# Cross entropy with label smoothing: load buffers moved to multiples of 256 bytes, the first row in three tiles instead of four, the second row loaded into the first row's buffers, the first row's finish moved

One core of one Trainium2 chip. The metric is the device time in microseconds of one execution (the median of several), compared with the kernel before on the same chip.

## The reference, cut to what matters

```python
batch, num_classes = 256, 32000
log_probs = logits - max(logits, row);  log_probs -= log(sum(exp(log_probs), row))
smooth_targets = smoothing / num_classes everywhere, plus 1 - smoothing at the label
loss = -sum(smooth_targets * log_probs, row)          # 256 float32
```

So each row needs the sum of its logits, the sum of their exps, and the logit at its label. The 32.77 MB of logits are read once. Each of the 128 partitions holds two batch rows of 32,000 columns, which the kernel works through one after the other ("first row", "second row").

## The kernel before

A tile of columns of all partitions is loaded; VectorE sums it (as two halves added with an accumulator), ScalarE takes exp with an accumulator. Both write a scratch result that nobody reads.

```python
WIDTHS = (
    (8000, 8000, 8000, 8000),
    (8000, 6272, 4736, 3648, 2688, 2048, 1536, 1216, 1024, 832),
)
RING_MIN = 4736
TURN_MAX = 3648
...
ring = ctx.enter_context(tc.tile_pool(name="ring", bufs=3))   # first pool: starts at byte 16,512
...
def load(w: int, col: int, name: str):
    if w >= RING_MIN:
        xt = ring.tile([P, max(WIDTHS[0])], FP32, name="xt", tag="xt")
    else:
        xt = tail.tile([P, w], FP32, name=name, tag=name)
    if col == 0:
        h = w // 2
        nc.sync.dma_start(out=xt[:, :h], in_=x[:, :h])
        nc.scalar.dma_start(out=xt[:, h:w], in_=x[:, h:w])
    else:
        nc.sync.dma_start(out=xt[:, :w], in_=x[:, col : col + w])
    return xt
...
# after the first row, before the second row's first tile:
#   GpSimd adds the four partial sums (half), ScalarE takes Ln (lse),
#   GpSimd finishes (lin, scaled, loss), TensorE turns the column, VectorE copies it
```

At the end of the second row a last Ln, two transposes on TensorE, two small VectorE operations and the store follow. Ten throw-away matrix products before that (20 matmul instructions in the trace) are meant to keep those transposes short: they take 0.27 us each here, where the first row's transpose, with no such products before it, took 0.37.

The softmax here doesn't subtract the row's maximum and nothing guards it: scores larger than these inputs give would overflow.

## Time and profile before

| | before |
|---|---|
| median of 6 runs | 84.78 us (84.75 to 84.93) |
| span of the profiled execution | 83.2 us |
| busy: DMA queues (sum of the three) / ScalarE / VectorE | 93.3% / 71% / 45% |
| last landing of a load / start of the final Ln | 79.11 us / 80.20 us |

The profiled execution itself took 84.96 us, 0.2 over the median. A "landing" is the last of the sixteen semaphore increments of a transfer, one from each DMA engine. A load runs on all sixteen engines; each engine moves eight partition rows of it, and each row is one packet. The lines that the argument rests on stand in the prediction.

### The profile page before, as it was taken

The page shows a single profiled execution, that of the slowest core. Times are in us where ns is not written, and L with a number is a line of the kernel's source. Part 1 is how long each engine was busy: PE and PEld are TensorE (multiplying, and loading weights), DVE is VectorE, ACT ScalarE, POOL GpSimd, SP SyncE. Part 2 cuts the span into 40 slices and gives each one's busy share as a digit, 9 for nine tenths or more (in the row PEclk, how much of TensorE's full clock was granted, in tenths as well). Part 3 has the DMA queues.
Part 4 walks back from the last instruction along what each step waited for, and adds up shares of the span by engine and source line. Part 5 has one row for each costly group of instructions (what it writes and reads, how often), then busy time and mean ns, then how long its engine had stood idle before and what let it go on. Part 6 is the DMA issues. An engine that isn't in the chain of part 4 may idle for free.

```text
span 83.2 us, 230 instructions
## 1 busy us (share of the span) xinstructions
PE 7.0 (8%) x23; PEld 5.0 (6%) x23; DVE 37.1 (45%) x35; ACT 58.8 (71%) x31; POOL 5.7 (7%) x19
## 2 busy tenths in 40 slices
PE   0000000000000000000000010000000000899020
PEld 0000000000000000000000000000000000787000
DVE  0000005950495009910397017922944736754860
ACT  5000005997499809994399908997999999999960
POOL 3201640031000000000000040000000000000000
PEclk9999999999999999999999999999999999999995
DMA  5999999997999899989998998998999999999600
GB/s 131 416 416 408 454 423 462 477 447 323 477 493 431 369 431 493 446 369 416 493 462 354 416 439 386 495 447 370 428 420 414 442 407 415 412 414 412 256 0 0
DMA packets 2258, 32.77 MB, mean 394 GB/s; under 512 B 337, under 2 KB 338, under 8 KB 850
## 3 DMA queue, kind: packets, MB, share of 16 engines
q1 hardware_dynamic: 2018, 30.72, 87.4%
q10 hardware_dynamic: 144, 2.05, 5.8%
q0 software_dynamic: 96, 0.00, 0.1%
HBM read 32.77 MB, written 0.00 MB: 394 GB/s over the span
## 4 chain that ended last, share of the span: by engine, by line
DMA 64%; ACT 32%; issue 1%; SPq 0%; PE 0%; DVE 0%; ACTq 0%
DMA xt<-in_logits_dram 40%; DMA xl<-in_logits_dram 23%; ACT ja L188 17%; ACT jt L188 15%; SPq L167 0%; PE lse_t L193 0%; DVE res L284 0%; ACT lse L279 0%; ACTq L188 0%
## 5 line engine op out<-in xcount | busy, mean ns | idle before, releaser
L188 ACT ACTIVATE ja<-xt 128x8000 bf16<-128x8000 f32 (+2 forms) x7 | 43.9, 6276 | 20.1 <-DMA xt<-in_logits_dram 20.0
L173 DVE SCALAR_TENSOR_TENSOR jd<-xt 128x4000 f32<-128x4000 f32 (+2 forms) x7 | 27.7, 3954 | 33.6 <-DMA xt<-in_logits_dram 33.6
L188 ACT ACTIVATE jt<-xl 128x3648 bf16<-128x3648 f32 (+6 forms) x7 | 12.2, 1748 | 0.1
L173 DVE SCALAR_TENSOR_TENSOR jd<-xl 128x1824 f32<-128x1824 f32 (+6 forms) x7 | 7.9, 1125 | 5.2 <-DMA xl<-in_logits_dram 5.0
L270 PE MATMUL warm<-xl,ident 128*128 128x256 f32 x20 | 6.1, 471 | 21.4 <-DMA xl<-in_logits_dram 21.4
L270 PEld LDWEIGHTS warm<-xl,ident 128*128 128x128 f32 x20 | 4.8, 246 | 22.5 <-DMA xl<-in_logits_dram 21.7
L193 PE MATMUL loss_t<-ident,loss 128*1 128x128 f32 x1 | 0.4, 372 | 49.2 <-POOL loss L224 49.2
L193 PEld LDWEIGHTS loss_t<-ident,loss 128*1 128x1 f32 x1 | 0.1, 79 | 49.2 <-POOL loss L224 49.2
L226 DVE COPY res<-loss_t 1x128 f32<-1x128 f32 x1 | 0.3, 278 | 4.5 <-PE loss_t L193 4.5
L211 POOL TENSOR_TENSOR half<-sums 128x4 f32<-128x4 f32 x1 | 0.2, 198 | 28.2 <-ACT ja L188 28.2
L125 POOL DMA_INDIRECT gat<-in_logits_dram,flat_idx x2 | 2.0, 1004 | 0.7 <-POOL ident masks.py:199 0.4
L92 ACT ACT_TABLE_LOAD x1 | 1.3, 1283 | 0.9 <-PEq L311 0.9
L188 ACT ACTIVATION_READ_ACCUMULATOR ja<-xt 128x1 f32 x7 | 1.3, 186 | 0.0
L188 ACT ACTIVATION_READ_ACCUMULATOR jt<-xl 128x1 f32 x7 | 1.3, 181 | 0.0
L146 POOL TENSOR_SCALAR weighted<-gat 128x1 f32<-128x1 f32 x1 | 0.8, 763 | 5.8 <-DMA gat<-in_logits_dram,flat_idx 5.8
L105 POOL DMA_DIRECT2D lab<-in_labels_dram x1 | 0.8, 766 | 1.0 <-POOLq L311 1.0
L216 ACT ACTIVATE lse<-half 128x1 f32<-128x1 f32 x1 | 0.2, 203 | 0.6 <-POOL half L211 0.6
L173 DVE DVE_READ_ACCUMULATOR jd<-xt 128x1 f32 x7 | 0.6, 82 | 0.0
L173 DVE DVE_READ_ACCUMULATOR jd<-xl 128x1 f32 x7 | 0.6, 82 | 0.0
L117 POOL TENSOR_TENSOR flat_idx<-rowoff,lab 128x2 int32<-128x2 int32 x1 | 0.2, 197 | 5.4 <-DMA lab<-in_labels_dram 5.4
L193 PE MATMUL lin_t<-ident,done 128*1 128x128 f32 x1 | 0.3, 270 | 3.0 <-DVE done L263 3.0
L282 DVE COPY lin_row<-lin_t 1x128 f32<-1x128 f32 x1 | 0.3, 278 | 0.4 <-PE lin_t L193 0.4
(20 smaller groups left out, 3.8 us busy)
## 6 DMA issues: line engine op xcount, KB each, us to landing
xt<-in_logits_dram SPq DMA_DIRECT2D x4, 4000.0 KB, 21.1
xt<-in_logits_dram SPq DMA_DIRECT2D x1, 3136.0 KB, 19.4
xt<-in_logits_dram SPq DMA_DIRECT2D x1, 2368.0 KB
xt<-in_logits_dram SPq DMA_DIRECT2D x1, 2000.0 KB, 11.5
xt<-in_logits_dram ACTq DMA_DIRECT2D x1, 2000.0 KB, 13.2
xl<-in_logits_dram SPq DMA_DIRECT2D x1, 1824.0 KB, 19.5
xl<-in_logits_dram SPq DMA_DIRECT2D x1, 1344.0 KB, 22.3
xl<-in_logits_dram SPq DMA_DIRECT2D x1, 1024.0 KB, 24.3
```

Of the source, the lines that this page charges most:

```text
L92: nc.scalar.add_instruction(mybir.InstLoadActFuncSet(name=nc.get_next_instruction_name(), act_func_set_id=tbl, ins=[], outs=[],))
L105: nc.gpsimd.dma_start(out=lab[:], in_=labels.bitcast(I32).rearrange("(p f) -> p f", p=P))
L117: nc.gpsimd.tensor_tensor(out=flat_idx[:], in0=rowoff[:], in1=lab[:].rearrange("p (r two) -> p r two", two=2)[:, :, 0:1], op=ALU.add,)
L125: nc.gpsimd.indirect_dma_start(out=gat[:, r : r + 1], out_offset=None, in_=logits[:], in_offset=bass.IndirectOffsetOnAxis(ap=flat_idx[:, r ...
L146: nc.gpsimd.tensor_scalar(out=weighted[r], in0=gat[:, r : r + 1], scalar1=label_weight, scalar2=None, op0=ALU.mult,)
L173: return nc.vector.scalar_tensor_tensor(out=jd[:, :h], in0=xt[:, :h], scalar=1.0, in1=xt[:, h:w], op0=ALU.mult, op1=ALU.add, accum_out=out,)
L188: nc.scalar.activation(out=ja[:, :w], in_=xt[:, :w], func=AF.Exp, accum_out=out)
L193: nc.tensor.transpose(out=row[:], in_=column, identity=ident[:])
L211: nc.gpsimd.tensor_tensor(out=half[:], in0=sums[:, :, :n], in1=sums[:, :, n:], op=ALU.add)
L226: nc.vector.tensor_copy(out=res[:, :, r : r + 1], in_=loss_t[:])
L270: nc.tensor.matmul(warm[:], lhsT=ident[:], rhs=xt[:, i * WARM_COLS : (i + 1) * WARM_COLS], start=True, stop=True,)
L282: nc.vector.tensor_copy(out=lin_row[:], in_=lin_t[:])
```

## The change

Four things at once. The load buffers are moved so that each starts on a multiple of 256 bytes (an unused pad of 384 bytes ahead of them; the first tile's split becomes a multiple of 64 columns). The first row comes in three tiles instead of four, the last of them large (the first tile is still loaded as two halves). The second row comes in eleven; nine of them are loaded into the first row's three buffers, several tiles to a buffer, and the last two have buffers of their own. And the finish of the first row moves behind the second row's first tile, with two scratch places instead of three. A beat is what a DMA engine moves in one cycle of its clock, 32 bytes. The intent: no lost beats in the transfers, and exp and loads in step to the end.

```diff
 WIDTHS = (
-    (8000, 8000, 8000, 8000),
-    (8000, 6272, 4736, 3648, 2688, 2048, 1536, 1216, 1024, 832),
+    (8000, 12480, 11520),
+    (8192, 6336, 4608, 3392, 2496, 1920, 1472, 1152, 960, 768, 704),
 )
-RING_MIN = 4736
-TURN_MAX = 3648
-WARM_LEFT, WARM_COLS = 5, 256
+FOLLOW = (1, 2, 6)
+TURN_MAX = 4608
+PAD = 384
+WARM_LEFT, WARM_COLS = 6, 256
...
-    ring = ctx.enter_context(tc.tile_pool(name="ring", bufs=3))
+    pad = ctx.enter_context(tc.tile_pool(name="pad", bufs=1))
+    pad.tile([nc.NUM_PARTITIONS, PAD // 4], FP32, name="pad", tag="pad")
+    wide = ctx.enter_context(tc.tile_pool(name="wide", bufs=1))
...
-    turn = ctx.enter_context(tc.tile_pool(name="turn", bufs=3))
+    turn = ctx.enter_context(tc.tile_pool(name="turn", bufs=2))
...
+    for r in range(R):                       # FOLLOW: how many second-row tiles share a buffer
+        for b in range(len(FOLLOW)):
+            ...
+            buf = wide.tile([P, w], FP32, name=f"wide{b}_{r}", tag=f"wide{b}")
+            ...buffers.append(buf[:, at : at + v])
...
-            h = w // 2
+            h = w // 128 * 64
...
+        if t == 0:                           # second row, after its first tile's exp
+            finish_first_row(part, exps)
```

## The prediction

> **What bounds the kernel now.** I read the page's 40 slices first, then the chain of work that ended last, then the tail of ScalarE's and VectorE's timeline, then the DMA records. The slices say which resource is never idle. The "DMA" row is the busy share of the 16 DMA engines in tenths:
>
> ```profile
> ACT  5000005997499809994399908997999999999960
> DMA  5999999997999899989998998998999999999600
> ```
>
> and the chain, as shares of the span by engine, is
>
> ```profile
> DMA 64%; ACT 32%; issue 1%; SPq 0%; PE 0%; DVE 0%; ACTq 0%
> ```
>
> The DMA engines are at 7 to 9 tenths from the second slice to the 37th (2.08 us each). ScalarE (exp) has holes through the first row and is full only in the last 13 slices. In the chain, 64% of the span is a transfer, 32% exp. The loads bound the kernel, and exp follows them closely at the end. How closely is in the timeline (start, duration, engine, line):
>
> ```profile
> 40.80 6.87 ACT L188 ACTIVATE ja<-xt 128x8000 bf16<-128x8000 f32 x1 [2.51 <-DMA xt<-in_logits_dram]
> 50.31 6.87 ACT L188 ACTIVATE ja<-xt 128x8000 bf16<-128x8000 f32 x1 [1.75 <-DMA xt<-in_logits_dram]
> 57.77 5.43 ACT L188 ACTIVATE ja<-xt 128x6272 bf16<-128x6272 f32 x1 [0.50 <-DMA xt<-in_logits_dram]
> ...
> 67.72 3.24 ACT L188 ACTIVATE jt<-xl 128x3648 bf16<-128x3648 f32 x1
> ...
> 70.96 2.44 ACT L188 ACTIVATE jt<-xl 128x2688 bf16<-128x2688 f32 x1
> ...
> 78.18 1.06 ACT L188 ACTIVATE jt<-xl 128x1024 bf16<-128x1024 f32 x1
> ...
> 79.24 0.88 ACT L188 ACTIVATE jt<-xl 128x832 bf16<-128x832 f32 x1
> ...
> 80.20 0.26 ACT L279 ACTIVATE lse<-elast,done 128x1 f32<-128x1 f32 x1
> ```
>
> The waits shrink from 2.51 to 0.50 us and then vanish, so the tile widths were already chosen so that each exp ends when the next tile lands. The trace's landing times (the last of a transfer's sixteen semaphore increments) show that the tail is still the loads': landings at 67.69, 70.94, 73.42, 75.31, 76.82, 78.10 and 79.11 us, exp starts 0.02 to 0.13 us after each. The final Ln starts at 80.20, and the rest (two transposes, one VectorE operation, the store) is not touched.
>
> Are transfers ever held up for a free buffer? No: the loads are issued at 20.35, 28.83, 38.32 and 47.79 us, each while one transfer is under way and at least one more is queued behind it; the DMA row never empties. The rate over two of the large transfers, the last column of the windows view, is
>
> ```profile
> 22.00:31.30 9.30, 0.00 (x0) 0.00 (x0) 4.19 (x2) 6.81 (x2) 0.00 (x0) 1.00 1.00 430
> 31.30:40.80 9.50, 0.00 (x0) 0.00 (x0) 4.33 (x2) 6.96 (x2) 0.00 (x0) 1.00 1.00 431
> ```
>
> **What the Trainium skill says.** (1) "DMA: Bandwidth & Descriptors", section "Where 436 GB/s comes from": 16 ports of 32 B at 850 MHz, 435 GB/s. The trace agrees: 430 to 431 above, so about 1% is left here. (2) Same page, "How a descriptor splits into AXI transactions": pieces of 256 B, each starting at a multiple of 256; a descriptor that starts off such a multiple begins at the boundary below and pays beats for bytes it does not use. (3) Same page, "Why small descriptors are slow": about 3 cycles fixed per packet. I tabulated the trace's DMA packets (one per partition row) by size. The shortest durations are 131 ns for 3,328 B, 404 for 10,752 B, 931 for 25,088 B, 1,185 for 32,000 B. The formula (bytes/32 + 3 + 4)/0.85 ns gives 130.6, 403.5, 930.6, 1184.7. The 4 is what a start 128 bytes past a boundary should cost (128/32 beats), and the kernel before does have all load buffers there: its first buffer is placed at byte 16,512 of a partition, 64.5 x 256, and the others follow in multiples of 256. The fit is within 1 ns on four sizes, but it cannot split 7 cycles into 3 and 4; that split is the page's. (4) "ScalarE: Activation LUTs", "What ACT_TABLE_LOAD costs": 186 ns + 0.833 ns per element. The rows by form give 6870 ns for 8000 columns (formula 6850) and 880 for 832 (879).
>
> **The change part by part.**
> *Alignment.* The pad of 384 bytes moves the first load buffer to 16,896 = 66 x 256; all widths are multiples of 64 columns, so all buffers are aligned, and the first split (3968 + 4032 columns instead of 4000 + 4000) aligns the second half at its source too. By point 2 each packet loses 4 cycles, 4.7 ns. There are 15 load transfers (the first is two halves), 8 packets on each engine per transfer, before and after alike: 120 x 4.7 ns = 0.56 us. The last landing goes from 79.11 to about 78.55.
> *Three transfers in the first row instead of four.* One transfer less before the row's end, one more after it; in the total nothing, at the row's end 8 packets of 7 cycles. The first row ends after 32 packets of 3 extra cycles instead of 40 of 7, plus one completion descriptor (about 15 ns) less: (280 - 96)/0.85 + 15 = 0.23 us earlier, so at 40.72 - 0.23 = 40.49 us.
> *Larger tiles in the first row.* The slack moves. The last first-row tile is 11,520 columns rather than 8000, so exp is now behind from 40.5 us on instead of from about 67. Exp steps: 0.833 ns per column, plus the overhead from one start to the next. The 1024-column step before took 79.24 - 78.18 = 1.06 us, of which 0.85 is columns, so 0.21; the mean of the last seven is 0.24, but those waited for landings. I take 0.20 to 0.24. The first step (same scratch written twice running, so it waits for the accumulator read) I put at 0.37, the last at 0.27 (832: 0.96 - 0.69). From 40.49 + 0.08: 43,520 columns x 0.8333 = 36.27; 0.37 + 10 x 0.20 + 0.27 = 2.64; the first row's Ln, now between the second row's first two tiles, 0.20 (its row: 203 ns). Sum: 79.68 us for the final Ln; with 0.24 per step 80.08.
> *Last tile 704 instead of 832 columns.* If the loads end it: 78.55 + 0.08 + 0.59 + 0.27 = 79.49.
> *Buffers that follow.* The second row's tiles go into the first row's three buffers. The 8192 can be issued at about 20.4, 6336 and 4608 when the exp of 12,480 is done (about 37.7), six more at about 50.5; the queue ahead lasts until 40.5, 50.2 and 63.1. No bubble.
> *Scratch 3 to 2, first row's finish moved.* Scratch at a distance of two is long free. The finish leaves the waiting point of 0.58 us (for GpSimd) out of ScalarE's queue, which was hidden before (1.75 us of waiting followed) and would not be now.
> *Sum.* The later of 79.49 (loads) and 79.68 to 80.08 (exp), against 80.20: 0.12 to 0.52 us saved. I choose the middle of the better half, 0.4, so 84.77 - 0.4 = 84.4.
>
> **The rivals.**
> A. *Alignment gives nothing*: the 7 cycles are fixed per packet. For it: the split is not seen in the trace, since every buffer was off by the same 128 bytes. Against: the page's rule fits without a free parameter. Then the row ends at 40.72 - 0.08 = 40.64, exp ends at 79.8 to 80.2, the loads at 79.11 + 0.94 = 80.05: 84.6 to 84.8.
> B. *Exp becomes the bound and eats the gain*: two tiles more in the unbroken chain. For it: my own sum has exp 0.2 to 0.6 us behind the loads. Against: the widths look tuned to keep step. Upper end 84.8.
> C. *False waits between slices of one buffer* (4608 waiting for the exp of 6336): that would stop prefetching and cost several us. Against: slices of one small tile are already written by several engines before, with no such wait in the list of waits. Would give 87 to 95; I give it 2%.
> D. *TensorE cools*: the warming products are 9 x 256 columns instead of 10 x 256 and end at about 75.6 instead of 77.0, with the last transposes near 80. The cold transpose takes longer:
>
> ```profile
> 49.21 0.37 PE L193 MATMUL loss_t<-ident,loss 128*1 128x128 f32 x1 [49.21 <-POOL loss L224]
> ...
> 80.52 0.27 PE L193 MATMUL lse_t<-ident,lse 128*1 128x128 f32 x1 [0.20 <-ACT lse L279]
> ```
>
> So at worst 0.1 us back; included as 0.03.
> E. *More than expected*: misaligned packets may also cause the slower ones (median 935 ns at 25,088 B where the shortest is 931). Removing those too gives up to 0.4 us more of loading, of which exp lets through only what comes before 40 us: 84.0.
>
> **Range and chances.** The centre is 84.4. B and A set the upper end near 84.8; E the lower near 84.0. A gain over 2% needs 83.07, that is 1.7 us; all DMA time above 435 GB/s is (busy 77.35 us, my sum of packet times over 16 engines, against 32.77 MB / 435 GB/s = 75.3) 2.0 us, and exp would have to give way too: 3%. A loss over 2% needs C: 2%.
>
> **What would show it right or wrong.** Right: the shortest packets at (bytes/32 + 3)/0.85, e.g. 935 ns for 25,344 B and 1,839 for 49,920; the first row's exp of 11,520 starting near 40.6; from there ScalarE without waits on a DMA above 0.1 us; the last landing near 78.6 and the final Ln near 79.7. Packets at 7 cycles mean rival A. Exp starts that trail their landings by more than 0.5 us mean B. Loads issued after the exp of a slice-mate mean C. A last transpose of 0.37 us means D. The prediction is wrong outright if the DMA row shows an empty slice before 78 us, or if the span moves more than 1 us either way.

## The result, and the profile after

| | before | after |
|---|---|---|
| median | 84.78 us | 84.30 us (84.21 to 84.64, 6 runs) |
| ratio of fast runs | 1 | 0.9945, 95% interval 0.9926 to 0.9963 |
| span of the profiled execution | 83.2 us | 82.4 us |
| last landing | 79.11 us | 78.53 us |
| start of the final Ln | 80.20 us | 79.50 us |

A ratio here is the mean time of one kernel's fast runs over that of the other's fast runs of the same rounds, so it is not quite the ratio of the medians. The change saves 0.5 us, 0.55%: within 2%, as forecast (84.4, range 84.0 to 84.8). The two profiled spans differ by more (0.8 us) because the profiled execution of before was 0.2 us over its median (84.96 us), that of after 0.1 under (84.22).

The same two rows of the slices and the chain, of the kernel after:

```profile
ACT  5000002999100999992399999999999999999960
DMA  6999999999998889988969969998999999999800
```

```profile
DMA 48%; ACT 47%; issue 1%; SPq 0%; PE 0%; DVE 0%; ACTq 0%
```

The DMA row still has no empty slice until the end. ScalarE's row is solid from the 21st slice rather than from the 29th, and the chain now splits evenly between loads and exp: from the first row's last tile on, it runs through exp. The timeline of ScalarE:

```profile
40.54 9.80 ACT L209 ACTIVATE ja<-wide 128x11520 bf16<-128x11520 f32 x1 [2.88 <-DMA wide<-in_logits_dram]
...
50.47 7.03 ACT L209 ACTIVATE ja<-wide 128x8192 bf16<-128x8192 f32 x1
...
57.50 0.19 ACT L250 ACTIVATE lse<-acc 128x1 f32<-128x1 f32 x1
57.69 5.48 ACT L209 ACTIVATE ja<-wide 128x6336 bf16<-128x6336 f32 x1
...
77.81 0.83 ACT L209 ACTIVATE jt<-tail 128x768 bf16<-128x768 f32 x1
...
78.64 0.77 ACT L209 ACTIVATE jt<-tail 128x704 bf16<-128x704 f32 x1
...
79.50 0.26 ACT L310 ACTIVATE lse<-elast,done 128x1 f32<-128x1 f32 x1
```

After the 2.88 us in front of the 11,520 there is no bracket, so no wait that the profile sees. Yet exp is hardly behind the loads: the trace's landings of the last five tiles (1472, 1152, 960, 768 and 704 columns) are at 74.14, 75.51, 76.69, 77.67 and 78.53 us, and their exps start 0.11 to 0.17 us later. Both keep step to the end.

**The packets.** I tabulated the trace's DMA packets and landings as for the prediction; the profile's printed views do not show them. A row of 25,344 bytes took 940 ns in 110 of its 128 packets, and up to 960 in the rest. Before, 25,088 bytes took 931 at the least, 935 in the median and up to 940. So the *shortest* packet is as far above its beats as before, 7 cycles, where I had said 3; what shrank is how many packets are longer than the shortest. By the test I had set myself this looks like rival A.

But the shortest duration is not the pace. The pace is in the landings: take the mean of the sixteen increments of a transfer, from the end of the first row to the last load. After: 78.38 - 40.28 = 38.10 us, that is 32,381 cycles at 850 MHz (38.095 us before rounding), where 32,000 columns are 32,000 beats for each engine (eight rows of 4 bytes a column, 32 bytes a beat). The trace itself gives that clock: from 2,816 to 49,920 bytes the shortest packets grow from 112 to 1,844 ns, 1.177 ns for 32 bytes. The 381 cycles over are shared by 11 transfers of 8 packets: 4.3 per packet. Before: 78.79 - 40.40 = 38.39 us, 629 cycles over, 80 packets: 7.9. So each packet did become about 3.5 cycles cheaper (7.86 - 4.33).

The mean of the recorded durations shows nearly the same: over the second row's tiles after its first, 10.2 cycles above the beats before, 7.2 after. In both kernels that is 2 to 3 cycles more than the pace, so by these records a packet starts before the one ahead of it is recorded as ended, whether aligned or not.

### The profile page after: what moved, and what is told of

Read it like the earlier page. It is cut to its first block, busy times and chain, and to the rows that moved or that the text cites. A ratio compares the mean times of both kernels' runs of the same rounds, so it can differ in the third digit from the quotient of the medians.

```text
span 82.4 us, 227 instructions
## 1 busy us (share of the span) xinstructions
PE 6.9 (8%) x21; PEld 4.9 (6%) x21; DVE 36.9 (45%) x35; ACT 58.1 (70%) x31; POOL 9.7 (12%) x19
## 4 chain that ended last, share of the span: by engine, by line
DMA 48%; ACT 47%; issue 1%; SPq 0%; PE 0%; DVE 0%; ACTq 0%
DMA wide<-in_logits_dram 48%; ACT ja L209 27%; ACT jt L209 19%; SPq L188 0%; PE lse_t L216 0%; DVE res L315 0%; ACT lse L310 0%; ACT lse L250 0%; ACTq L209 0%
## 5 line engine op out<-in xcount | busy, mean ns | idle before, releaser
L209 ACT ACTIVATE ja<-wide 128x8000 bf16<-128x8000 f32 (+4 forms) x5 | 39.8, 7958 | 20.7 <-DMA wide<-in_logits_dram 20.7
L194 DVE SCALAR_TENSOR_TENSOR jd<-wide 128x4000 f32<-128x4000 f32 (+11 forms) x12 | 34.4, 2870 | 38.9 <-DMA wide<-in_logits_dram 38.9
L209 ACT ACTIVATE jt<-wide 128x4608 bf16<-128x4608 f32 (+6 forms) x7 | 14.6, 2093 | 0.0
L301 PE MATMUL warm<-wide,ident 128*128 128x256 f32 x18 | 6.0, 508 | 11.6 <-DMA wide<-in_logits_dram 11.6
L236 POOL TENSOR_TENSOR acc<-acc,sums 128x2 f32<-128x2 f32 x1 | 4.1, 4127 | 12.6 <-ACT ja L209 12.6
L301 PEld LDWEIGHTS warm<-wide,ident 128*128 128x128 f32 x18 | 4.7, 267 | 12.8 <-DMA wide<-in_logits_dram 11.9
L209 ACT ACTIVATE jt<-tail 128x768 bf16<-128x768 f32 (+1 forms) x2 | 1.6, 800 | 0.0
L209 ACT ACTIVATION_READ_ACCUMULATOR jt<-wide 128x1 f32 x7 | 1.3, 187 | 0.0
L194 DVE SCALAR_TENSOR_TENSOR jd<-tail 128x384 f32<-128x384 f32 (+1 forms) x2 | 1.1, 542 | 0.0
L194 DVE DVE_READ_ACCUMULATOR jd<-wide 128x1 f32 x12 | 1.0, 81 | 0.0
```

The lines of the kernel that those rows point to most:

```text
L194: return nc.vector.scalar_tensor_tensor(out=jd[:, :h], in0=xt[:, :h], scalar=1.0, in1=xt[:, h:w], op0=ALU.mult, op1=ALU.add, accum_out=out,)
L209: return nc.scalar.activation(out=ja[:, :w], in_=xt[:, :w], func=AF.Exp, accum_out=out)
L236: nc.gpsimd.tensor_tensor(out=acc[:], in0=total, in1=sums[:, :, t : t + 1], op=ALU.add)
L301: nc.tensor.matmul(warm[:], lhsT=ident[:], rhs=xt[:, i * WARM_COLS : (i + 1) * WARM_COLS], start=True, stop=True,)
```

## The experiments

Twelve kernels ran, in three groups on three chips; each group shares the runs of the kernel before (medians 84.90, 84.84 and 84.89 us). "Over" is the pace just described: cycles per packet over the beats, second row. "Start" is where the load buffers start, in bytes past a multiple of 256.

| run | start | median us | ratio to before, 95% | last landing us | over |
|---|---|---|---|---|---|
| before | 128 | 84.78 | 1 | 79.11 | 7.9 |
| after | 0 | 84.30 | 0.9945 (0.9926 to 0.9963) | 78.53 | 4.3 |
| a1_before_aligned | 0 | 84.29 | 0.9929 (0.9909 to 0.9950) | 78.59 | 4.3 |
| a2_after_off128 | 128 | 84.76 | 0.9987 (0.9968 to 1.0006) | 79.03 | 7.9 |
| a3_after_off64 | 64 | 84.78 | 0.9993 (0.9969 to 1.0017) | 79.15 | 7.8 |
| a4_after_off192 | 192 | 84.65 | 0.9981 (0.9959 to 1.0002) | 78.88 | 7.9 |
| b1_src_off128 | 0, source at 128 | 84.34 | 0.9935 (0.9921 to 0.9949) | 78.54 | 3.7 |
| b2_src_dst_off128 | 128, source at 128 | 84.69 | 0.9982 (0.9969 to 0.9996) | 78.99 | 7.4 |
| c1_finish_early | 0 | 84.57 | 0.9969 (0.9953 to 0.9984) | 78.55 | 4.8 |
| c2_ln_first | 0 | 88.56 | 1.0441 (1.0425 to 1.0457) | 78.50 | 3.9 |
| d1_half_pieces | 128, one end on a multiple | 84.53 | 0.9953 (0.9938 to 0.9968) | 78.81 | 5.6 |
| d2_exp_half | 0 | 84.30 | 0.9925 (0.9907 to 0.9943) | 78.60 | 4.2 |
| d3_turn3 | 0 | 84.32 | 0.9932 (0.9915 to 0.9948) | 78.49 | 3.9 |
| d4_split_4000 | 0 | 84.23 | 0.9919 (0.9902 to 0.9937) | 78.53 | 4.0 |

(The last landing also depends on how far apart the sixteen engines finish, 0.27 us in a4 and 0.43 to 0.56 in a1 to a3; the pace does not.)

### Which part of the change is it?

**a1**: the kernel before with the alignment alone.

```diff
+    pad = ctx.enter_context(tc.tile_pool(name="pad", bufs=1))
+    pad.tile([nc.NUM_PARTITIONS, 384 // 4], FP32, name="pad", tag="pad")
     ring = ...
-            h = w // 2
+            h = w // 128 * 64
```

> The kernel before with only the 384-byte pad and the aligned first split. Alignment theory (each load packet costs 4 cycles of 0.85 GHz less, 120 packets on each DMA engine, so 0.56 us): last load lands at about 78.55 us instead of 79.11, exp keeps up (its back-to-back overhead is 0.19 us per tile), final Ln near 79.5, time 84.3, 0.5 us under the kernel before. Rival (the gain comes from the widths, the fewer early transfers and the smaller last tile): landings as before, 84.8.

Measured: 84.29 us, and 4.3 cycles over per packet. The whole gain is there without any of the new widths, shared buffers or moved finish. (The final Ln of its profile, of an execution of 84.42 us, is at 79.69 rather than the 79.5 expected.)

**a2**: the changed kernel with the alignment alone taken away.

```diff
-PAD = 384
+PAD = 256
```

> The changed kernel with a pad of 256 bytes, which puts every load buffer 128 bytes past a multiple of 256 again, all else as changed. Alignment theory: last landing near 79.1, time 84.7 to 84.9, the gain is gone; packets spread over several ns again. Rival (widths): 84.3, as the changed kernel.

Measured: 84.76 us; its ratio to before has 1 inside the interval. ScalarE, VectorE and all widths are the same as after; only the start of the buffers differs. The pace is back at 7.9 and the spread too (25,344 bytes: 940 at the least, 945 in the median, 948 at most). a1 and a2 together settle it: alignment gives all of the gain that can be measured, the rest together nothing that the runs can tell from zero. Something small is not excluded: a2's interval leaves room for 0.27 us, and the smaller last tile does bring the final Ln nearer to the last landing (0.97 us after it in a2, 1.09 before).

### What is it about the alignment?

My reason was that a packet pays beats for the bytes below its start. Then the distance must count.

**a3** and **a4**: `PAD = 192` and `PAD = 320`, all else as changed.

> The changed kernel with all load buffers 64 bytes past a multiple of 256. Rule of wasted beats (a packet pays for the bytes below its start): 64/32 = 2 cycles per packet, 120 packets, 0.28 us: last landing 78.8, time 84.55. Rival (any start off the multiple costs the same, one more piece): last landing 79.1, time 84.8.

> The changed kernel with all load buffers 192 bytes past a multiple of 256. Rule of wasted beats: 192/32 = 6 cycles per packet, 0.85 us over the changed kernel: last landing 79.4, time 85.1. Rival (any start off the multiple costs the same): last landing 79.1, time 84.8.

Measured: 7.8 and 7.9 over, like 128 bytes, and 84.78 and 84.65 us. The rule of wasted beats wanted 2 and 6 more cycles than aligned; it falls. Any of the three starts costs the same, 3.5 cycles per packet. (In all three kernels the ends of the rows are off by as much as the starts.)

**b1** and **b2**: move the source instead (b1), or both (b2).

```diff
-    (8000, 12480, 11520),
-    (8192, 6336, ..., 768, 704),
+    (8032, 12480, 11488),
+    (8224, 6336, ..., 768, 672),
     # buffers still rounded up to a multiple of 256 bytes; b2 has PAD = 256 as well
```

> The changed kernel with the first tile of each row 32 columns wider and the last 32 narrower, load buffers still at multiples of 256 bytes: the source in memory of 12 of the 14 later transfers (96 of 120 packets on each engine) now starts 128 bytes past such a multiple, the destination does not. If only the destination counts: 84.3, last landing 78.5, all packets of a size equal. If source and destination count alike: about 4 cycles on 96 packets, 0.45 us: 84.7, last landing 79.0.

> The same columns with the pad of 256 bytes: source and destination both 128 bytes past a multiple of 256. If only the destination counts: 84.75, as with the destination alone. If what counts is that the two are shifted against each other: 84.3. If both count and add: 85.2.

Measured: b1 is as fast as the changed kernel (84.34 us, 3.7 over, all packets of a size equal), b2 is as slow as with the destination alone (84.69, 7.4). Where the row starts in memory, counted from the start of the logits (their own address is in no trace), does not matter here; where it lies in the partition does. Nor does it help that both are shifted alike. (In b2 a packet of 32,896 or 2,688 bytes, which starts 128 past a multiple and *ends* on one, has the same median as in b1. That led to d1.)

**d1**: buffers off by 128 bytes, but tile widths such that one end of nearly every row lies on a multiple, so that no row is cut into more pieces of 256 bytes than its length needs.

```diff
-    (8000, 12480, 11520),
-    (8192, 6336, 4608, 3392, 2496, 1920, 1472, 1152, 960, 768, 704),
-TURN_MAX = 4608
-PAD = 384
+    (8032, 12480, 11488),
+    (8224, 6304, 4640, 3360, 2528, 1888, 1504, 1120, 992, 768, 672),
+TURN_MAX = 4640
+PAD = 256
-            h = w // 128 * 64
+            h = w // 128 * 64 + 32
```

> All load buffers 128 bytes past a multiple of 256 (pad of 256 bytes), but nearly all tiles an odd number of 32 columns wide, so that a row that starts 128 past a multiple ends on one, and the next slice starts on one: off the boundary, yet never cut into more pieces of 256 bytes than its length needs (104 of 120 packets on each engine; 12,480 and 768 columns stay as they were). Theory (the cost is that of one more piece): last landing 78.6, 84.3 to 84.4. Rival (a start off the boundary costs by itself): some 64 of 120 packets start off it, last landing 78.8 to 78.9, 84.6; if an end off it costs as well, 84.8.

Measured: 84.53 us, halfway, and 5.6 over. My theory of the extra piece wanted 84.3 and about 4.3, and falls. The last of the forecasts (start and end each cost) said 84.8, too much. The first rival, that a start off a multiple costs by itself, has the time (84.6) and the landing right, but not tile by tile. Single tiles scatter (in the aligned kernels from about 2 to 7 over, by the place of the transfer in the order), so I compare means, at the same places:

| cycles over per packet | d1 | aligned kernels | a2 to a4 |
|---|---|---|---|
| start off, end on a multiple (8224, 6304, 3360, 1888, 1120) | 5.6 | 3.6 | 8.1 |
| start on, end off (4640, 2528, 1504, 992) | 6.1 | 4.1 | 8.3 |

(The aligned kernels here are after, c2, d2, d3 and d4.) An end off a multiple costs what a start does. What fits all the runs is a price per end of a row that is off a multiple of 256 bytes in the partition, some 2 cycles each. This rule was made after d1, and no run was made to test it; but earlier runs hold tiles with one end off whose pace it was not made from. In b1 the tiles of 8224 and 11,488 columns start on a multiple and end off one (5.9 and 6.1 over); in b2 they start off and end on (6.0 and 5.4). In the aligned kernels these places have 2.8 and 2.5, in a2 to a4 8.0 and 8.5. What the engine does at such an end, no run here shows.

**d4**: the first tile split 4000 + 4000 again, in the aligned kernel.

> The changed kernel with its first tile split 4000 + 4000 again instead of 3968 + 4032. One piece more on 8 of 120 packets at most, 0.04 us: not to be told from 84.3.

Measured: 84.23 us. As expected, not to be told apart; that line of the diff is worth nothing measurable.

### What do the other parts do?

**c1**: the finish of the first row put back before the second row's first tile on all engines (`finish_first_row` called ahead of the loop, without the two orderings).

> The changed kernel with the whole finish of the first row put back before the second row's first tile, on all engines. Theory (exp has no slack after the first row, so GpSimd's sum and the Ln stand in its way): the exp of 8192 starts near 51.05 us instead of 50.47, final Ln 0.4 us later, 84.7. Rival (the loads bind in the end and hide it): 84.3. Here VectorE waits too, so GpSimd's sum should take about 0.2 us.

Measured: 84.57 us against 84.34 for b1, an aligned kernel of the same group, and 84.30 for the changed kernel: the order matters, by 0.2 to 0.3 us rather than 0.4. The timeline:

```profile
50.20 0.19 ACT L209 ACTIVATION_READ_ACCUMULATOR ja<-wide 128x1 f32 x1
...
50.52 0.20 POOL L236 TENSOR_TENSOR acc<-acc,sums 128x2 f32<-128x2 f32 x1 [12.62 <-ACT ja L209]
50.74 0.20 ACT L249 ACTIVATE lse<-acc 128x1 f32<-128x1 f32 x1 [0.36 <-POOL acc L236]
50.79 0.19 POOL L241 TENSOR_TENSOR lin<-acc,weighted 128x1 f32<-128x1 f32 x1
50.85 7.01 ACT L209 ACTIVATE ja<-wide 128x8192 bf16<-128x8192 f32 x1
...
79.80 0.26 ACT L308 ACTIVATE lse<-elast,done 128x1 f32<-128x1 f32 x1
```

ScalarE waits 0.36 us for GpSimd, and the exp of 8192 starts at 50.85 instead of 50.47. Nothing after it makes that up: the final Ln starts at 79.80 instead of 79.50. In the kernel before, the same order cost nothing, since 1.75 us of waiting for a load followed (a1 has it too, and is as fast as after). The new widths create this cost and the moved finish removes it.

**c2**: only the Ln put ahead of that exp; VectorE still sums the 8192 columns first.

```diff
+        if t == 0:
+            finish_first_row(part)        # between sum_logits and sum_exps; the Ln without its ordering
```

> The changed kernel with only the first row's Ln put ahead of the exp of 8192 in ScalarE's queue; VectorE still sums the 8192 columns before its copy. Theory (GpSimd's addition really is held up for 4.1 us while VectorE's sum of two operands runs, as the trace of the changed kernel shows it): Ln at about 54.8, exp of 8192 from 55.0, final Ln 4.3 us later, time 88.5. Rival (the 4.1 us is a wrong record, GpSimd's spans being rough): like the early finish, 84.7.

Measured: 88.56 us, the only run far from the rest. In the trace of the changed kernel one addition on GpSimd of 128 x 2 elements, elsewhere 0.19 us, is shown as 4.13 us long:

```profile
37.74 0.19 POOL L236 TENSOR_TENSOR acc<-sums 128x2 f32<-128x2 f32 x1 [16.21 <-ACT ja L209]
50.57 4.13 POOL L236 TENSOR_TENSOR acc<-acc,sums 128x2 f32<-128x2 f32 x1 [12.63 <-ACT ja L209]
```

It ends with VectorE's sum of 8192 columns (50.22 to 54.65 there). The same in c2, where ScalarE now stands behind it:

```profile
50.17 4.42 DVE L194 SCALAR_TENSOR_TENSOR jd<-wide 128x4096 f32<-128x4096 f32 x1 [3.49 <-DMA wide<-in_logits_dram]
...
50.53 4.12 POOL L236 TENSOR_TENSOR acc<-acc,sums 128x2 f32<-128x2 f32 x1 [12.63 <-ACT ja L209]
...
54.68 0.20 ACT L249 ACTIVATE lse<-acc 128x1 f32<-128x1 f32 x1 [4.28 <-POOL acc L236]
...
54.79 7.01 ACT L209 ACTIVATE ja<-wide 128x8192 bf16<-128x8192 f32 x1
```

ScalarE waited 4.28 us, so the long record is real. This is what the Trainium skill, "SBUF — State Buffer", section "Who interferes with whom", says: a VectorE instruction with two inputs from that memory contends with a GpSimd instruction that reads it, as the second input comes through a shared interface. Here it held GpSimd up for 4.1 us. In c1 VectorE stands behind the copy at that moment, and the same addition takes 0.20 us. So the order of the changed kernel hides a 4 us block: the Ln comes at 57.50 us, when the sum has been ready since 54.70.

**d2**: exp over half the columns of every tile but the last (a wrong result, relative error 0.06).

```diff
+        k = w if w == WIDTHS[1][-1] else w // 2
-        ... out=ja[:, :w], in_=xt[:, :w] ...
+        ... out=ja[:, :k], in_=xt[:, :k] ...
```

> The changed kernel with exp over only half the columns of every tile but the last (wrong result on purpose, same transfers): takes ScalarE off the path until the last tile. Both bind in the changed kernel (exp starts trail their landings by 0.1 us in the tail): final Ln at 78.53 + 0.08 + 0.59 + 0.27 = 79.47, 84.25 to 84.3, no gain. Rival (exp is the bound and hides more of the gain): 84.0 or less.

Measured: 84.30 us, and the final Ln at 79.56. With half the exp, nothing is gained: the loads bind in the end. c1 shows the other side: exp delayed by 0.38 us costs 0.2 to 0.3. Both bind at once, which is what tuned widths look like.

**d3**: three scratch places again, `TURN_MAX = 3392` so that they fit.

> The changed kernel with three scratch places again (for tiles up to 3392 columns, to fit). The scratch was free long before with two: 84.3, exp steps unchanged at 0.19 us beyond the columns. Rival (two places make exp wait for its own writes): 84.1.

Measured: 84.32 us; exp steps as after. The number of scratch places is worth nothing either way. In this profile and in d4's (and c2's) the last two transposes took 0.37 us each instead of 0.27; the page's row of granted clocks has 6 tenths (c2: 5) in the 39th slice, in which they lie, where after has 9. The granted clock can't be all of it, as the first row's transpose took 0.37 in a slice of 9 tenths (before); the cause stays open.

```profile
79.94 0.37 PE L216 MATMUL lse_t<-ident,lse 128*1 128x128 f32 x1 [0.19 <-ACT lse L310]
```

In the profile of after it took 0.27. So rival D of the prediction does occur in some executions, at 0.1 us for one transpose.

No run is faster than the changed kernel beyond the noise; a1 and d4 are level with it.

## Why the prediction was right, and where a step of it was not

- **Alignment, 0.56 us off the last landing (79.11 to 78.55).** Right in size: 78.53 measured, 78.59 in a1 where it is alone, and lost again in a2. Nearly right in the pace: 3.5 cycles per packet (7.9 to 4.3) for the 4 predicted, 0.50 us over 120 packets. **Wrong in the reason.** The step "4 is what a start 128 bytes past a boundary should cost (128/32 beats)" failed: 64 and 192 bytes cost the same as 128, and the cost sits at both ends of a row, about 2 cycles each. That the size came out right is luck: at 128 bytes the wrong rule gives 4 cycles and two ends gave 3.5, but at 64 or 192 bytes it would have given 2 or 6. The fit within 1 ns on four sizes was no evidence for it, since 7 cycles fit just as well with aligned buffers: the fit was made on the shortest durations, which do not change. So the test that I named ("shortest packets at (bytes/32 + 3)/0.85") would have misjudged the change.
- **"Full only in the last 13 slices"** (ScalarE, before). The row shown has nines in the ten slices from the 29th to the 38th; nothing rests on the difference.
- **2.0 us of DMA time above 435 GB/s.** This was summed from recorded durations, which overlap. By the pace I estimate 120 packets of 7.9 cycles over, 1.1 us: less was there to be gained than I said.
- **End of the first row at 40.49 us.** Right: the 11,520 columns landed at 40.46 and their exp began at 40.54 (predicted 40.57). The 15 ns in that sum for one completion descriptor was worked out from no trace; the traces record packets of 4 bytes, 16 to a transfer, at 9 ns. It is too small to matter here.
- **Exp chain, final Ln at 79.68 to 80.08.** Somewhat too late: 79.50. The term that was off is the overhead per tile, put at 0.20 to 0.24 us. In the unbroken chain it is 0.18 to 0.20 (768 columns: 78.64 - 77.81 = 0.83, of which 0.64 is columns), and the first step cost 0.33 instead of 0.37.
- **Loads' end, final Ln at 79.49.** It came at 79.50; d2 shows that this is the end that binds when exp is made light.
- **The widths.** I had them as part of a sum; a1 is level with the changed kernel without them, so they contribute nothing that can be measured. That they are needed to keep exp in step when the first row comes in fewer transfers was not tested.
- **The moved finish.** I saw that 0.58 us of waiting for GpSimd would no longer be hidden (c1: 0.2 to 0.3 us is what it costs), and missed that GpSimd's addition would take 4.1 us; it is harmless only because the Ln was put behind the exp.
- **Rivals.** A (alignment gives nothing) is refuted by a1 and a2. B (exp eats the gain) by the exps starting at most 0.17 us after their landings in the tail. C (false waits between slices of a buffer) did not come: the loads follow one another without a gap. D occurs in some executions. E (the slower packets vanish) is what the records show: their mean fell from 10.2 to 7.2 cycles above the beats while the shortest stayed at 7. It goes with nearly the whole gain and is no addition to it, since the shortest packets lost nothing.

## What to carry to other kernels

When a kernel is bound by many row-wise loads, look at where the destination rows start and end in the partition: multiples of 256 bytes at both ends saved 3.5 cycles on each packet here, 0.5 us over 120 packets on each engine, for the price of an unused pad. Judge a change in transfers by the spacing of their landings, not by the durations of packets: the shortest did not change at all, and even their mean in d1 (7.8 above the beats, with 7.2 after and 10.2 before) shows less of the cost than the pace does. And before a small GpSimd operation is put on ScalarE's path, see whether VectorE is then in a long operation with two operands.

## What the Trainium skill lacked or had wrong

- "DMA: Bandwidth & Descriptors", "How a descriptor splits into AXI transactions": the rule that a start off a multiple of 256 bytes pays for the bytes below it does not describe these loads. On the source side it cost nothing (3.7 cycles over per packet with 12 of 14 sources off by 128 bytes, 4.3 without). On the destination side 64, 128 and 192 bytes cost the same (7.8, 7.9, 7.9), and an end off a multiple costs as a start does (5.6 to 6.1 with one of the two).
- The same page, "Why small descriptors are slow", has about 3 cycles fixed per packet; aligned rows here keep a pace of 3.9 to 4.8 cycles over the beats per packet. That the recorded duration of a packet (at least 7 over) is longer than its share of the pace is on no page.
- "SBUF — State Buffer", "Who interferes with whom": right, but without a figure for an instruction with an accumulator; here an addition of 128 x 2 elements on GpSimd took 4.13 us instead of 0.19 behind a sum of 4096 + 4096 columns.
- "ScalarE: Activation LUTs", "What ACT_TABLE_LOAD costs": its 186 ns + 0.833 ns per element holds for single instructions (6.87 us for 8000). For instructions back to back it has an overlap of about 93 ns, which would leave 0.09 us over the columns; with an accumulator read between them the spacing here is 0.18 to 0.20 us over, which is on no page that I read.
